# The low parts of the gated delta net's weights: all of them on VectorE

## The chip, the core and the metric

The kernel runs on one core of a Trainium2 chip. The metric is the time of the program on the device, in microseconds. In the profile PE is TensorE's matmuls, PEld its weight loads, DVE is VectorE, ACT is ScalarE, POOL is GpSimd and SP is SyncE, which here only issues DMAs. TensorE's clock has two levels, 2.4 GHz (granted clock 1.0) and 1.2 GHz (0.5).

## What is computed

The reference is a model of four layers on 256 tokens of width 1024. Each layer is a SwiGLU feed-forward part, a mixer, and another feed-forward part; the mixers are an S5, an HGRN2, a gated delta net and a MoBA attention. The change touches the third mixer alone:

```python
def _gdn_mixer(x, w_in, conv_w, a_log, dt_bias, norm_g, w_out):
    qkv, z, beta_raw, a_raw = jnp.split(x @ w_in, [...], axis=-1)
    qkv = jax.nn.silu(_causal_conv(qkv, conv_w))
    q, k, v = jnp.split(qkv, [Hk * dk, 2 * Hk * dk], axis=-1)
    q, k = l2norm(q) * dk ** -0.5, l2norm(k)
    # per chunk: a triangular system, then a scan over the chunks
    sol = triangular_solve(m + eye(C), rhs, lower=True, unit_diagonal=True)
    _, o = lax.scan(step, S0, (...))
    o = _rms(o, norm_g) * jax.nn.silu(z)
    return o @ w_out
```

## The kernel before

Every product with a weight is made from two parts of each factor. A unit of weights is a tile of 128x1024 numbers. It arrives in float32 (`raw`, by SP's DMAs). ScalarE rounds it to TensorE's format (`hi`, line 88), a second engine makes the rest, `lo = raw - hi` (line 91), and TensorE adds up three products, hi by hi, hi by lo and lo by hi. Where the weights are the stationary factor these are lines 315 to 317 (`mm3`, 24 matmuls of 256 columns for a unit), where they move, lines 347 to 349 (`wide`, 12 matmuls of 512 columns).

`Weights.pump` prepares up to four units ahead of the one that TensorE takes next: `hi` and `lo` have four buffers each, and so has `raw`. VectorE makes `lo`, but for units whose number is in the set `aside`: those go to GpSimd. `plan_gdn` puts every second unit of the gated delta net (`GDN_ASIDE = 2`) into that set, 33 of 65.

The gated delta net works in four quarters of four value heads. For each quarter, `project` makes keys and queries (convolution in `conv`, lines 1389 to 1398, tiles `xr`, `cy`, `th`, `kq`; then the norm, an inverse square root of seven to eleven small VectorE instructions on a tile of 128x8, lines 261 to 266 and 1426, tiles `grn_r` and `grn_t`, which TensorE spreads at line 1430). `invert` builds and inverts the triangular matrices (lines 1465 to 1559; GpSimd has four instructions in it, lines 1471, 1477, 1492 and 1508). `values`, `read` (with a second inverse square root, tiles `gf_r` and `gf_t`), `turn`, `gate` and `out` follow. The quarters are interleaved in the code.

The order of the instructions on each engine comes from a scheduler at build time, which goes by its own idea of when things are ready; the code fixes it only where it says `keep_in_program_order`. So a change of the engine of some instructions can give a new order of all the others. On the chip each engine runs its own list in that order.

Of the kernel before, what the change touches and what calls it, by code (L numbers as in the profile page):

```python
# [9 lines left out]
F32 = mybir.dt.float32  # L10
# [3 lines left out]
OP = mybir.AluOpType  # L14
# [5 lines left out]
D_FF = 2816  # L20
FT = D_FF // 128
EPS = 1e-6
GDN_ASIDE = 2
PREP = (2, 16)
WARM = (14, 14, 8)

# [1 line left out]
def as_ap(ap, offset, dims):  # L28
    return bass.AP(tensor=ap.tensor, offset=ap.offset + offset, ap=dims)


class Weights:
# [6 lines left out]
    def __init__(self, nc, raw, split):  # L39
        self.nc, self.raw, self.split = nc, raw, split  # L40
        self.blocks, self.units = [], []
        self.loaded = self.ready = self.taken = 0
        self.tiles, self.parts = {}, {}
        self.aside = set()

    def block(self, srcs, k0, nk, units):

# [28 lines left out]
    def pump(self, most=HL, pin=lambda ins: ins):  # L76
        while True:
            low = min((b for b, _ in self.units[self.ready:self.ready + 8]), default=len(self.blocks))
            if self.loaded < min(len(self.blocks), low + self.RAW):
                self._load()  # L80
            elif self.ready < min(len(self.units), self.taken + most):
                b, (k0, nk, c0, ncol) = self.units[self.ready]
                src = self.tiles[b][:, k0:k0 + nk, c0:c0 + ncol]
                hi = self.split.tile([128, nk * ncol], F32R, tag="hi", name="hi")
                lo = self.split.tile([128, nk * ncol], F32R, tag="lo", name="lo")
                hi = hi.rearrange("p (k c) -> p k c", k=nk)
                lo = lo.rearrange("p (k c) -> p k c", k=nk)
                pin(self.nc.scalar.copy(hi, src))  # L88

                eng = self.nc.gpsimd if self.ready in self.aside else self.nc.vector  # L90
                eng.tensor_tensor(lo, src, hi.bitcast(F32), op=OP.subtract)  # L91
                self.parts[self.ready] = (hi, lo)
                self.ready += 1
            else:
                return
# [8 lines left out]
class Model:  # L104
# [1137 lines left out]

    def plan_gdn(self, i):
        I = self.I
        first = len(self.w.units)
        n = 6176
        w_in = as_ap(I["gdn_w_in"], 0, [[n, D], [1, n]])
        self.w.units += self.w.block([(w_in, n - 128, 128)], 0, KT, [(0, KT, 0, 128)])
        w_out = as_ap(I["gdn_w_out"], 0, [[D, 2 * D], [1, D]])

        def kq(q):
            self.w.cols(w_in, D + q * 256, 256)
            self.w.cols(w_in, q * 256, 256)

        kq(0)
        for q in range(4):
            self.w.cols(w_in, 2 * D + q * 512, 512)
            if q < 3:
                kq(q + 1)
            self.w.wide([(w_in, 4 * D + q * 512, 512)], 0, KT)  # L1260
            if q > 1:
                self.plan_out(w_out, 4 * (q - 2), 4)
        for q in (2, 3):
            self.plan_out(w_out, 4 * q, 4)
        self.w.aside |= set(range(first, len(self.w.units), GDN_ASIDE))

    def gdn_consts(self, pool, i):
        nc, I = self.nc, self.I
# [556 lines left out]
```

## Time and profile before

| | us |
|---|---|
| median of 3 runs | 2255.6 (2252.84 to 2257.62) |
| the profiled execution | 2255.48 |
| its span, first to last instruction | 2253.7 |
| the stretch in which GpSimd makes low parts, 1237 to 1571 us of the span | 334 |

The profiled execution is 0.1 us from the median of the runs, and 1.8 us of it lie outside the span. Over the whole span TensorE is busy 95%, VectorE 65%, ScalarE 51% and GpSimd 13%. A row of groups gives the line, the engine, the operation, tiles as out<-in, shapes, the count, then the busy time in us and the mean of one in ns, then the idle time of that engine just before them and what ended it. A row of waits reads: who waited, for whom, us in all, times, the longest one.

### The profile page before, as it was taken

Reading aid. Unit: us, or ns where it says so; the run is one execution under the profiler, and the core shown is the slowest. Engines: PE = TensorE matmul, PEld = TensorE weight load, DVE = VectorE, ACT = ScalarE, POOL = GpSimd, SP = SyncE. Lnnn points to the kernel's source line nnn. Section 1 sums busy time; section 2 is a strip of 40 time slices with the busy share of each in tenths; the row PEclk is TensorE's granted clock in tenths of the full one; section 3 lists DMA queues with packets and bytes.
Section 4 is the critical chain, followed back from the end, with each engine's and each line's share of the span. In section 5 each row is a group of like instructions: output and inputs, shape, how many; then the busy total and the mean of one; then the engine's idle time right before and its main releaser. Section 6 shows DMA issues by size and latency. Waiting matters only on the chain.

```text
span 2253.7 us, 30309 instructions
## 1 busy us (share of the span) xinstructions
PE 2147.5 (95%) x11480; PEld 1771.5 (79%) x11480; DVE 1464.5 (65%) x2412; ACT 1159.8 (51%) x1876; POOL 288.1 (13%) x305
## 2 busy tenths in 40 slices
PE   8989888999999999999999888899999999999998
PEld 6767566888888888887888766777888888898886
DVE  7986675556555877557554888887655555666555
ACT  6444344445454755445444566764544544555443
POOL 0598600000000000001000422322000000000000
PEclk9999899999999999999999999999999999999999
DMA  8656956655555645555655433233555655555553
GB/s 254 195 188 203 239 185 166 191 195 179 186 179 185 198 132 169 187 190 167 190 185 175 144 100 104 85 113 121 179 187 172 202 186 178 196 168 178 187 177 103
DMA packets 317906, 389.63 MB, mean 173 GB/s; under 512 B 14192, under 2 KB 247856, under 8 KB 316736
## 3 DMA queue, kind: packets, MB, share of 16 engines
q1 hardware_dynamic: 314768, 383.92, 53.7%
q10 hardware_dynamic: 2800, 3.68, 0.9%
q8 instruction: 90, 1.47, 0.3%
q14 instruction: 56, 0.46, 0.1%
q0 software_dynamic: 192, 0.10, 0.0%
HBM read 375.65 MB, written 12.01 MB: 172 GB/s over the span
## 4 chain that ended last, share of the span: by engine, by line
PE 80%; DVE 9%; ACT 4%; DMA 3%; POOL 2%; issue 1%; SPq 0%; ACTq 0%; DVEq 0%; POOLq 0%
PE acc L349 23%; PE acc L347 23%; PE acc L348 23%; DVE lo L91 2%; PE acc L315 2%; PE acc L316 2%; PE acc L317 2%; PE aux L439 2%; DVE cy L1395 1%; DMA raw<-in_ffn_w_up_dram 1%; ACT hi L88 1%; PE aux L230 1%; POOL s5e L733 1%; POOL s5e L734 1%; POOL s5tmp L732 1%
## 5 line engine op out<-in xcount | busy, mean ns | idle before, releaser
L91 DVE TENSOR_TENSOR lo<-raw,hi 128x1024 fp32r<-128x1024 f32 x648 | 813.1, 1257 | 585.4 <-ACT hi L88 582.3
L88 ACT CAST hi<-raw 128x1024 fp32r<-128x1024 f32 x681 | 713.1, 1049 | 708.2 <-PE acc L349 657.5
L347 PE MATMUL acc<-hi,xhl 128*128 128x512 f32 x1568 | 627.2, 400 | 9.9 <-ACT hi L88 9.4
L348 PE MATMUL acc<-lo,xhl 128*128 128x512 f32 x1568 | 618.9, 395 | 2.8 <-DVE lo L91 2.7
L349 PE MATMUL acc<-hi,xhl 128*128 128x512 f32 x1568 | 616.9, 394 | 0.0
L347 PEld LDWEIGHTS acc<-hi,xhl 128*128 128x128 f32 x1568 | 297.1, 190 | 73.0 <-ACT hi L88 10.7
L349 PEld LDWEIGHTS acc<-hi,xhl 128*128 128x128 f32 x1568 | 296.9, 189 | 66.6 <-issue 3.1
L348 PEld LDWEIGHTS acc<-lo,xhl 128*128 128x128 f32 x1568 | 297.5, 190 | 64.4 <-DVE lo L91 5.2
L347 PE MATMUL acc<-hi,hhl 128*128 128x512 f32 x704 | 276.9, 393 | 0.0
L349 PE MATMUL acc<-hi,hhl 128*128 128x512 f32 x704 | 276.7, 393 | 0.0
L348 PE MATMUL acc<-lo,hhl 128*128 128x512 f32 x704 | 275.5, 391 | 0.0
L349 PEld LDWEIGHTS acc<-hi,hhl 128*128 128x128 f32 x704 | 132.8, 189 | 27.6
L348 PEld LDWEIGHTS acc<-lo,hhl 128*128 128x128 f32 x704 | 132.9, 189 | 27.4
L347 PEld LDWEIGHTS acc<-hi,hhl 128*128 128x128 f32 x704 | 132.7, 188 | 27.0
L317 PE MATMUL acc<-xhl,lo 128*128 128x256 f32 x520 | 150.2, 291 | 0.0
L316 PE MATMUL acc<-xhl,hi 128*128 128x256 f32 x520 | 149.5, 290 | 0.2 <-DVE xhl L241 0.2
L315 PE MATMUL acc<-xhl,hi 128*128 128x256 f32 x520 | 149.6, 291 | 0.1
L427 ACT ACTIVATE sl<-acc,norm_r 128x256 f32<-128x256 f32 x176 | 83.6, 475 | 107.2 <-PE acc L349 88.9
L91 POOL TENSOR_TENSOR lo<-raw,hi 128x1024 fp32r<-128x1024 f32 x33 | 81.8, 2478 | 342.7 <-ACT hi L88 322.6
L430 DVE TENSOR_TENSOR h<-acc,sl 128x256 f32<-128x256 f32 x176 | 74.0, 420 | 49.8 <-ACT sl L427 49.7
L315 PEld LDWEIGHTS acc<-xhl,hi 128*128 128x128 f32 x520 | 99.6, 193 | 2.6 <-issue 1.7
L316 PEld LDWEIGHTS acc<-xhl,hi 128*128 128x128 f32 x520 | 99.8, 193 | 1.6 <-issue 0.9
(564 smaller groups left out, 2285.7 us busy)
## 6 DMA issues: line engine op xcount, KB each, us to landing
raw<-in_ffn_w_gate_dram SPq DMA_DIRECT2D x174, 512.0 KB, 3.9
raw<-in_ffn_w_up_dram SPq DMA_DIRECT2D x174, 512.0 KB, 4.8
raw<-in_ffn_w_down_dram SPq DMA_DIRECT2D x80, 1024.0 KB, 4.9
raw<-in_gdn_w_in_dram SPq DMA_DIRECT2D x24, 1024.0 KB, 5.2
raw<-in_hg_w_in_dram SPq DMA_DIRECT2D x16, 1024.0 KB, 5.3
raw<-in_moba_w_in_dram SPq DMA_DIRECT2D x12, 1024.0 KB, 5.0
raw<-in_ffn_w_down_dram SPq DMA_DIRECT2D x16, 512.0 KB, 3.7
raw<-in_s_w_glu_dram SPq DMA_DIRECT2D x16, 512.0 KB, 5.2
```

The costliest lines, as they stand in the source:

```text
L88: pin(self.nc.scalar.copy(hi, src))
L91: eng.tensor_tensor(lo, src, hi.bitcast(F32), op=OP.subtract)
L230: nc.tensor.transpose(q[:, j * 128:j * 128 + 128], self.x[:, t, k * 128:k * 128 + 128], self.ident)
L315: t.matmul(p, hi, ah, start=first, stop=False)
L316: t.matmul(p, hi, al, start=False, stop=False)
L317: t.matmul(p, lo, ah, start=False, stop=last)
L347: mm(p, ah, hi[:, j], start=first and j == 0, stop=False)
L348: mm(p, ah, lo[:, j], start=False, stop=False)
L349: mm(p, al, hi[:, j], start=False, stop=last and j == n - 1)
L427: nc.scalar.activation(sl, p[:, :256], AF.Silu, scale=self.r_col[:, t:t + 1])
L430: return nc.vector.tensor_tensor(waiting[-1][1][:, t], p[:, 256:], sl, op=OP.mult)
L439: nc.tensor.transpose(q[:, c:c + 128], h[:, t, f * 128:f * 128 + 128], self.ident)
```

## The change

The set `aside` and the constant `GDN_ASIDE` go, and line 91 always uses VectorE (it becomes line 87; lines behind it move up by four to six).

```diff
-                eng = self.nc.gpsimd if self.ready in self.aside else self.nc.vector
-                eng.tensor_tensor(lo, src, hi.bitcast(F32), op=OP.subtract)
+                self.nc.vector.tensor_tensor(lo, src, hi.bitcast(F32), op=OP.subtract)
...
     def plan_gdn(self, i):
         I = self.I
-        first = len(self.w.units)
...
-        self.w.aside |= set(range(first, len(self.w.units), GDN_ASIDE))
```

No instruction is added or lost: 33 move from GpSimd's list to VectorE's, and the scheduler orders the gated delta net anew on all engines. Before that stage and behind it the lists are the same.

GpSimd in the middle of the gated delta net, before: low parts (`lo`) stand between the four instructions of `invert` for each quarter.

```order
L91 TENSOR_TENSOR lo<-raw,hi 128x1024 x2
L1508 COPY e<-gd_e 128x256
L1477 TENSOR_TENSOR gd<-gd,beta 128x1024
L91 TENSOR_TENSOR lo<-raw,hi 128x1024 x2
L1492 AFFINE_SELECT nt<-nt 128x1024
L91 TENSOR_TENSOR lo<-raw,hi 128x1024
L1471 AFFINE_SELECT gd<-gd 128x1024
```

The same place now:

```order
L1502 COPY e<-gd_e 128x256
L1471 TENSOR_TENSOR gd<-gd,beta 128x1024
L1486 AFFINE_SELECT nt<-nt 128x1024
L1465 AFFINE_SELECT gd<-gd 128x1024
```

GpSimd keeps four instructions for each quarter, 16 in the stage, and nothing stands between them.

VectorE in the inverse square root of the first quarter's keys and queries, before (`grn_r` and `grn_t` are its small tiles, `cy` is the convolution, and line 1426 is what TensorE's line 1430 waits for):

```order
L265 SCALAR_TENSOR_TENSOR grn_t<-grn_t,gmc 128x8
L1395 SCALAR_TENSOR_TENSOR cy<-xr_10012,gd_w,cy 128x256
L266 SCALAR_TENSOR_TENSOR grn_r<-grn_t,grn_r 128x8
L1395 SCALAR_TENSOR_TENSOR cy<-xr_10012,gd_w,cy 128x256
L264 TENSOR_TENSOR grn_t<-grn_r 128x8
L91 TENSOR_TENSOR lo<-raw,hi 128x1024
L265 SCALAR_TENSOR_TENSOR grn_t<-grn_t,gmc 128x8
L1395 SCALAR_TENSOR_TENSOR cy<-xr_10012,gd_w,cy 128x256
L266 SCALAR_TENSOR_TENSOR grn_r<-grn_t,grn_r 128x8
L1389 TENSOR_TENSOR xr_10012<-acc,r_row 128x256
L1426 TENSOR_SCALAR grn_r<-grn_r 128x8
```

The same stretch now:

```order
L87 TENSOR_TENSOR lo<-raw,hi 128x1024
L261 SCALAR_TENSOR_TENSOR grn_t<-grn_t,gmc 128x8
L1389 SCALAR_TENSOR_TENSOR cy<-xr_10012,gd_w,cy 128x256
L262 SCALAR_TENSOR_TENSOR grn_r<-grn_t,grn_r 128x8
L87 TENSOR_TENSOR lo<-raw,hi 128x1024
L260 TENSOR_TENSOR grn_t<-grn_r 128x8
L1392 SCALAR_TENSOR_TENSOR cy<-th,cy 128x256
L261 SCALAR_TENSOR_TENSOR grn_t<-grn_t,gmc 128x8
L1383 TENSOR_TENSOR xr_10012<-acc,r_row 128x256
L262 SCALAR_TENSOR_TENSOR grn_r<-grn_t,grn_r 128x8
L87 TENSOR_TENSOR lo<-raw,hi 128x1024
L1420 TENSOR_SCALAR grn_r<-grn_r 128x8
```

Three low parts stand in these rows, and a fourth just ahead of them, where one stood in the whole chain; line 1420 is what line 1426 was.

VectorE where the stage begins, before: the residual sum `x` of the feed-forward part ahead and the split of its transposed result `xhl`, which TensorE's first products of the stage read.

```order
L484 SCALAR_TENSOR_TENSOR x<-acc,half,x 128x512
L241 SCALAR_TENSOR_TENSOR xhl<-aux,gains,xhl 128x128 x2
L91 TENSOR_TENSOR lo<-raw,hi 128x1024
L241 SCALAR_TENSOR_TENSOR xhl<-aux,gains,xhl 128x128
L484 SCALAR_TENSOR_TENSOR x<-acc,half,x 128x512
L241 SCALAR_TENSOR_TENSOR xhl<-aux,gains,xhl 128x128
L91 TENSOR_TENSOR lo<-raw,hi 128x1024
```

The same place now:

```order
L480 SCALAR_TENSOR_TENSOR x<-acc,half,x 128x512
L237 SCALAR_TENSOR_TENSOR xhl<-aux,gains,xhl 128x128
L87 TENSOR_TENSOR lo<-raw,hi 128x1024
L237 SCALAR_TENSOR_TENSOR xhl<-aux,gains,xhl 128x128
L87 TENSOR_TENSOR lo<-raw,hi 128x1024
L237 SCALAR_TENSOR_TENSOR xhl<-aux,gains,xhl 128x128
L87 TENSOR_TENSOR lo<-raw,hi 128x1024
L480 SCALAR_TENSOR_TENSOR x<-acc,half,x 128x512
L237 SCALAR_TENSOR_TENSOR xhl<-aux,gains,xhl 128x128
L87 TENSOR_TENSOR lo<-raw,hi 128x1024
```

Three low parts instead of one stand ahead of the second sum of `x`, for which TensorE's transposes wait.

## Rows read from the trace of the kernel before

**Rows 1.** Stretches (us: length, PE, PEld, DVE, ACT, POOL busy; clock, DMA).

```profile
1237.00:1571.00 334.00, 291.96 (x2175) 241.37 (x2174) 272.68 (x567) 206.84 (x453) 101.17 (x49) 0.96 0.34 108
1000.00:1237.00 237.00, 234.74 (x1068) 193.25 (x1067) 134.26 (x205) 114.00 (x157) 6.18 (x13) 1.00 0.57 184
```

**Rows 2.** Waits of TensorE from 1237 to 1571 us.

```profile
PE aux L1430 <- DVE grn_r L1426: 5.9, 2, 4.0
PE aux L1552 <- DVE lo L1547: 5.5, 2, 3.3
...
PE acc L316 <- DVE xhl L241: 0.2, 1, 0.2
```

**Rows 3.** Chain that ended last, 1237 to 1571: shares, longest pieces (start, us, what).

```profile
by line: DVE cy L1395 9.5%; issue 5.5%; PE acc L349 5.1%; PE acc L348 5.1%; PE acc L347 5.0%; DVE lo L91 4.4%; ACT zb L1518 3.3%; ACT hi L88 3.0%; PE aux L1574 2.8%; PE acc L316 2.6%; PE acc L315 2.5%; PE acc L317 2.3%; DVE kq L1398 2.3%; D
...
1293.75 4.12 DVE cy L1395 x4
...
1384.58 3.20 DVE lo L91
```

**Rows 4.** Groups of GpSimd from 1237 to 1571 us, the first.

```profile
L91 POOL TENSOR_TENSOR lo<-raw,hi 128x1024 fp32r<-128x1024 f32 x33 | 81.8, 2478 | 342.7 <-ACT hi L88 322.6 <-PE aux L1516 20.0
```

**Rows 5.** Groups of VectorE from 1237 to 1571 us.

```profile
L1395 DVE SCALAR_TENSOR_TENSOR cy<-xr,gd_w,cy 128x256 f32<-128x256 f32 x96 | 63.3, 666 | 5.0 <-ACT cy L1392 4.4
L91 DVE TENSOR_TENSOR lo<-raw,hi 128x1024 fp32r<-128x1024 f32 x33 | 44.9, 1360 | 8.1 <-ACT hi L88 8.0
...
L1398 DVE SCALAR_TENSOR_TENSOR kq<-th,cy 128x256 f32<-128x256 f32 x16 | 12.6, 786 | 0.6 <-ACT th L1397 0.5
...
L261 DVE TENSOR_SCALAR grn_r<-gmc 128x8 int32<-128x8 int32 x4 | 7.4, 1842 | 0.1
L1398 DVE SCALAR_TENSOR_TENSOR cy<-th,cy 128x256 f32<-128x256 f32 x16 | 7.1, 446 | 2.9 <-ACT th L1397 2.9
...
L262 DVE TENSOR_SCALAR gf_r<-gf_r 128x8 int32<-128x8 int32 x4 | 5.0, 1239 | 0.1
L265 DVE SCALAR_TENSOR_TENSOR gf_t<-gf_t,gm 128x8 f32<-128x8 f32 x12 | 4.2, 346 | 0.2
...
L264 DVE TENSOR_TENSOR grn_t<-grn_r 128x8 f32<-128x8 f32 x12 | 3.6, 297 | 0.2
```

**Rows 6.** The low parts on VectorE from 1000 to 1237 us, ahead of the stage.

```profile
L91 DVE TENSOR_TENSOR lo<-raw,hi 128x1024 fp32r<-128x1024 f32 x81 | 99.1, 1225 | 86.3 <-ACT hi L88 86.2
```

**Rows 7.** VectorE in order of time (start, us, what), from 1272 us.

```profile
1275.03 1.78 DVE L264 TENSOR_TENSOR grn_t<-grn_r 128x8 f32<-128x8 f32 x1
...
1277.45 0.17 DVE L264 TENSOR_TENSOR grn_t<-grn_r 128x8 f32<-128x8 f32 x1
...
1278.46 0.48 DVE L1395 SCALAR_TENSOR_TENSOR cy<-xr,gd_w,cy 128x256 f32<-128x256 f32 x1
...
1278.93 1.22 DVE L91 TENSOR_TENSOR lo<-raw,hi 128x1024 fp32r<-128x1024 f32 x1
1280.07 2.31 DVE L265 SCALAR_TENSOR_TENSOR grn_t<-grn_t,gmc 128x8 f32<-128x8 f32 x1
```

**Rows 8.** GpSimd in order of time, the same place.

```profile
1274.88 1.90 POOL L1477 TENSOR_TENSOR gd<-gd,beta 128x1024 f32<-128x1024 f32 x1
1279.02 3.33 POOL L91 TENSOR_TENSOR lo<-raw,hi 128x1024 fp32r<-128x1024 f32 x1 [2.23 <-ACT hi L88]
```

**Rows 9.** TensorE in order of time, the same place.

```profile
1283.53 0.77 PE L1430 MATMUL aux<-ident,grn_r 128*128 128x128 f32 x2 [4.00 <-DVE grn_r L1426]
```

**Rows 10.** Two stretches with a lower granted clock (the eighth column).

```profile
1280.00:1300.00 20.00, 14.48 (x89) 13.57 (x89) 14.96 (x27) 8.02 (x18) 7.09 (x4) 0.83 0.31 91
...
1440.00:1460.00 20.00, 15.32 (x107) 11.53 (x108) 17.75 (x35) 9.80 (x19) 4.82 (x3) 0.74 0.35 106
```

**Rows 11.** Waits around the parts of the weights, 1237 to 1571 us.

```profile
ACT hi L88 <- PE acc L349: 32.1, 16, 4.8
...
DVE lo L91 <- ACT hi L88: 8.0, 6, 3.1
```

More of the change, by code (lines that the diff above doesn't have):

```diff
@@ L22 @@
 EPS = 1e-6
-GDN_ASIDE = 2
 PREP = (2, 16)
@@ L43, in __init__ @@
         self.tiles, self.parts = {}, {}
-        self.aside = set()
     def block(self, srcs, k0, nk, units):
```

## The prediction

> **What bounds the kernel now.** I read the stretches first, to see which engine has time to give. From 1237 to 1571 us TensorE is idle for 334 - 292.0 = 42.0 us, while in the 237 us ahead of it it is idle for 2.3 us [rows 1]. So a change in this stage can give back some 42 us at most, and what the granted clock hides besides. VectorE is busy 272.7 us there, 82%, more than any engine but TensorE. Next come TensorE's waits, to see who ends them. 13 kinds of them end at a VectorE instruction, and they sum to 32.9 us; the two longest and the shortest are shown [rows 2] (`lo` of line 1547 is a tile of the inversion, not a part of a weight). No wait of TensorE in the stretch ends at a part of a weight, made by either engine. So what TensorE waits for is VectorE's small work on keys, queries and inverses.
>
> Then the groups of VectorE, to see whether it works or stands. The small steps of the inverse square roots have means of 300 to 1840 ns [rows 5], and in order of time one and the same step takes 1.78 us at one place and 0.17 us at another [rows 7]. The step that takes 2.31 us starts at 1280.07 and ends at 1282.38, and GpSimd's low part runs from 1279.02 to 1282.35 [rows 7, 8]. The one that takes 1.78 us ends at 1276.81, and another instruction of GpSimd ends at 1276.78 [rows 7, 8]. So VectorE's instruction is held until GpSimd's ends, and is still counted as busy. TensorE's gap of 4.00 us, up to 1283.53, stands right behind these two [rows 9]. The chain tells the same: its longest pieces in the stretch are such held instructions, at 1293.75 and 1384.58 us for instance [rows 3].
>
> **What the change removes.** The held time, group by group, as busy time less count times the quiet duration: `cy` 63.3 - 96 x 0.48 = 17.2; `kq` 12.6 - 16 x 0.446 = 5.5 (quiet: the other group of the same line); `grn_r` 7.4 - 4 x 0.17 = 6.7; `gf_r` 5.0 - 4 x 0.17 = 4.3; low parts 44.9 - 33 x 1.225 = 4.5; and five groups of twelve small steps each, from 4.2 down to 3.6 us, some 19.8 - 60 x 0.17 = 9.6 [rows 5 to 7]. That is 47.8 us. GpSimd's low parts are 81.8 of its 101.2 busy us there [rows 1, 4], 81%, so 39 us of the held time by share. If the other instructions held nothing it would be 48, but one of them does [rows 8]. I take 42, near the share, since the low parts are also the longest.
>
> The Trainium skill has this as a rule (SBUF — State Buffer, section Who interferes with whom): VectorE and GpSimd share a pair of ports as an exclusive lock, and an instruction of VectorE with two inputs in SBUF is held by one of GpSimd that reads SBUF. By that rule the 16 instructions that GpSimd keeps go on holding VectorE, since they read SBUF too. The trace agrees: the 1.78 us step stood behind one of them. So the 47.8 - 42 us are not counted as gain.
>
> **What it adds.** 33 low parts on VectorE at 1.225 us [rows 6] are 40.4 us; they follow each other at 1.14 us [rows 7], which would make 37.6. I take 40.4. So VectorE's load falls by 42 - 40.4 = 2 us only: it is not relieved. What counts is where the two kinds of time lie.
>
> Held time lies on the path nearly always, because one hold of 2 us puts its own instruction there: I take 90%, 38 us. For low parts the chain has 4.4% of 334 = 14.7 us of the 44.9 that they are busy [rows 3, 5], 33%, which is one bound, 13 us of 40.4; 90%, 36 us, is the other. In the new order three more of them than before stand in the first quarter's inverse square root, which TensorE's line 1430 waits for, so they are nearer to that path than the present ones; I take 60%, 24 us.
>
> A low part on VectorE also waits for its `hi`, and now all of VectorE's list waits with it. The present 33 wait 8.0 us in all [rows 11]. Another 33 at that rate add 8 us of standing, 60% of it on the path: 5 us; the bounds are nothing (the scheduler puts them where `hi` is long done) and 8. GpSimd has such waits today, 322.6 us [rows 4], but that is idle time of an engine with nothing queued behind it except its own four instructions a quarter.
>
> **The clock.** Behind TensorE's gaps the granted clock falls: in three stretches of 20 us it is 0.83, 0.83 and 0.74 (two shown) [rows 10], one of them right behind the gap that ends at 1283.53. Against 1.0 that is 3.4 + 3.4 + 5.2 = 12 us. If the held instructions go and a part of the gaps with them, I count a third back, 4 us; the bounds are 0 and 12.
>
> **What costs nothing.** GpSimd's list gets short; the 16 instructions left start earlier or at the same time. The order of SP's transfers moves in a few places, but no wait of TensorE for weights shows in the stretch. The lists before and behind the stage are unchanged.
>
> **The sum.** -38 + 24 + 5 - 4 = -13 us against the profiled execution, 2255.5, which is as good as the median (2255.6). Forecast: 2242.5 us.
>
> **The rivals.** *The whole gain.* The new low parts lie like the present ones, in the gaps of VectorE's own path: -38 + 13 + 0 - 8 = -33, so 2222 us. For it: TensorE's 32.9 us behind VectorE and the 12 us of clock leave room for it. Against it: the order above shows low parts inside a chain that TensorE waits for.
>
> *An even trade.* VectorE is bound by its load, 82% busy, and its load falls by 2 us while the new order neither helps nor hurts: 2253 us, within 0.2% (4.5 us, about what a measurement of this kernel can tell from no change). For it: the two sums, 42 and 40.4. Against it: it takes held time and low parts for equally harmful, while the chain has 33% of the one and nearly all of the other.
>
> *Slower: VectorE's list stands behind ScalarE's.* ScalarE's `hi` waits for TensorE to free a buffer, 32.1 us in 16 times behind line 349 [rows 11]. With GpSimd out, every such wait passes through `hi` and a low part into VectorE's one list, behind which the convolutions and the inverse square roots queue, and TensorE waits for these. Then 90% of the low parts and all of the standing lie on the path, the clock gives nothing, and the first sum of the stage stands behind three low parts instead of one, 2.4 us: -38 + 36 + 8 + 2.4 = +8.4, so 2264 us. It decides from where over (38 - 8) / 40.4, some three quarters, of the low parts' time lands on the path. For it: the new order puts low parts among the steps of chains. Against it: a low part of 1.2 us is shorter than a hold of some 2 us, and the order puts it where the scheduler thinks `hi` ready, while a hold falls on whatever is just there.
>
> The Trainium skill has a rule that speaks for this side (Perfetto Trace Analysis, section Optimizing Scalar/DVE Operations): with VectorE saturated, giving some of its work even to GpSimd may make sense, though the two share a port and it might not help. By its first half nothing is saved and the added time alone counts, +24 + 5, so 2284 us; the held time in this trace stands against that, and I give it no more than the tail above the range.
>
> That the change doesn't do what it says is out: the new lists show no low part on GpSimd.
>
> **How the numbers follow.** Forecast, from 5 to 24 us faster: 0.42. The whole gain: 0.16. The even trade: 0.20. Slower: 0.22. Faster by over 0.2% is 0.58, within 0.2% is 0.20, slower 0.22. The range reaches to the rivals on both sides, 2222 to 2265, and leaves out about a tenth at either end. The forecast's own range is 2231 to 2250.
>
> **What would show it.** In the profile after: the small steps back at 0.17 us but for a few beside GpSimd's 16 instructions, `cy` near 0.48 and `kq` near 0.45; VectorE's busy time in the stage about the same, with 66 low parts in it; TensorE idle 20 to 30 us instead of 42, and fewer stretches with a lower clock. The forecast is wrong in its main step if the held time goes and TensorE's idle time stays: then low parts stand in the chain of waits where the held steps stood. It is wrong in its first step if the small steps stay long without GpSimd beside them. If VectorE's idle time before low parts grows far beyond 8 + 8 us, the slower rival is at work.

## The result, and the profile after

The changed kernel takes 2225.2 us (median of four runs, 2221.2 to 2227.2), the kernel before in the same comparison 2255.0. The ratio is 0.9865, 95% interval 0.9846 to 0.9884: 30 us faster. The forecast was 13 us faster, 2242.5. The direction and the place were right, and the time lies inside the range, near its lower end; the size was less than half of what came.

The profiled execution took 2227.2 us with a span of 2225.5, 28.2 us under the span before. First the stage and the stretch ahead of it, as in [rows 1] (window, length, busy time of PE, PEld, DVE, ACT and POOL, granted clock, DMA). The window 1239 to 1545 answers to 1237 to 1571 of before.

```profile
1239.00:1545.00 306.00, 287.48 (x2187) 238.51 (x2186) 261.53 (x602) 207.01 (x455) 19.95 (x16) 0.97 0.40 121
```
```profile
1000.00:1239.00 239.00, 236.74 (x1070) 194.66 (x1069) 134.36 (x206) 113.95 (x157) 6.17 (x13) 0.99 0.57 184
```

The whole difference lies in the stage: 334 us became 306. TensorE's idle time there went from 42.0 us to 306 - 287.5 = 18.5, which is 23.5 of the 28; its busy time fell by the other 4.5. The clock accounts for about as much: 0.04 x 334 - 0.03 x 306 = 4.2 us, roughly, since both clocks are rounded to 0.01. The 20 us windows with a lower clock that are left (compare [rows 10]):

```profile
1360.00:1380.00 20.00, 17.41 (x141) 13.20 (x140) 15.96 (x42) 13.55 (x29) 2.51 (x2) 0.83 0.33 105
...
1420.00:1440.00 20.00, 18.31 (x132) 12.01 (x132) 18.25 (x44) 16.13 (x34) 2.52 (x2) 0.86 0.22 62
1440.00:1460.00 20.00, 19.87 (x120) 15.97 (x119) 15.87 (x36) 6.99 (x9) 0.00 (x0) 0.97 0.62 204
...
1520.00:1540.00 20.00, 13.89 (x69) 10.69 (x68) 15.05 (x37) 5.92 (x13) 0.00 (x0) 0.83 0.34 105
```

The window that held the gap of [rows 9] is at 1.00 now. But there are four windows under 1.00, and there were four before: beside the three that the forecast counted there is this one.

```profile
1300.00:1320.00 20.00, 16.15 (x123) 11.44 (x124) 14.52 (x25) 15.55 (x35) 4.76 (x2) 0.92 0.45 145
```

By the forecast's reckoning (what is missing to 1.0, times 20 us) the four lose 10.2 us now and lost 13.6 before. The groups of VectorE and the first of GpSimd in the stage, to be laid beside [rows 4, 5]:

```profile
L87 DVE TENSOR_TENSOR lo<-raw,hi 128x1024 fp32r<-128x1024 f32 x66 | 80.5, 1220 | 8.8 <-ACT hi L86 8.7
L1389 DVE SCALAR_TENSOR_TENSOR cy<-xr,gd_w,cy 128x256 f32<-128x256 f32 x96 | 46.6, 493 | 0.2
...
L1392 DVE SCALAR_TENSOR_TENSOR kq<-th,cy 128x256 f32<-128x256 f32 x16 | 6.9, 430 | 4.4 <-ACT th L1391 4.4
...
L257 DVE TENSOR_SCALAR grn_r<-gmc 128x8 int32<-128x8 int32 x4 | 2.0, 498 | 0.0
...
L262 DVE SCALAR_TENSOR_TENSOR gf_r<-gf_t,gf_r 128x8 f32<-128x8 f32 x12 | 1.8, 154 | 0.1
```
```profile
L1471 POOL TENSOR_TENSOR gd<-gd,beta 128x1024 f32<-128x1024 f32 x4 | 7.6, 1898 | 44.2 <-ACT gd L1470 41.3 <-issue 2.9
```

The groups that were long are back at or near their quiet durations: `cy` 666 to 493 ns, `kq` 786 to 430, the small steps to 154. The `grn_r` of line 257 is the exception, with 498 ns (1842 before): one of its four took 1.52 us and ended at 1275.42, and GpSimd's product with `beta` ended at 1275.39. By the forecast's own reckoning (busy time less count times quiet duration) `cy` keeps 0.5 us of its 17.2 and `grn_r` 1.3 of its 6.7. So VectorE does 33 more low parts in less busy time, 261.5 us for 272.7. Its waits for `hi` are 8.7 us for 66 low parts, where they were 8.0 for 33 [rows 11].

TensorE's waits, all that the view lists (compare [rows 2]), and the chain of the stretch (compare [rows 3]):

```profile
PE aux L1646 <- DVE goo L1643: 6.1, 1, 6.1
PE aux L1516 <- ACT zb L1512: 3.4, 8, 0.7
PE aux L1409 <- ACT csq L1408: 2.8, 3, 1.4
PE aux L1534 <- DVE zz L1530: 2.5, 2, 1.7
PE aux L1357 <- DVE gg L1353: 1.0, 1, 1.0
PE aux L1424 <- DVE grn_r L1420: 1.0, 1, 1.0
PE aux L1439 <- DVE cy L1392: 0.8, 1, 0.8
```
```profile
by line: issue 25.4%; ACT hi L86 6.5%; ACT zb L1512 6.4%; PE acc L343 5.5%; PE acc L345 5.4%; PE acc L344 5.2%; PE acc L311 2.1%; PE acc L312 2.1%; ACT dg L1493 2.0%; PE aux L1568 1.9%; PE acc L313 1.8%; ACT gd L1470 1.8%; ACT gj L1587 1.6%
```

The waits behind VectorE sum to 11.4 us where they were 32.9, and over half of that is one wait for `goo` at the end of the stage. That wait is hardly the low parts' doing: it is still 5.3 us in the run below that leaves all 33 out. No wait ends at a low part. In the chain `cy` led with 9.5% and low parts had 4.4%; now no line of VectorE is among the thirteen of 1.6% and more. Added up piece by piece, low parts have 4.8 us of the chain now, with 66 of them on VectorE, and had 14.6 with 33. But a quarter of this chain is "issue", time whose cause the profile does not show, so that the low parts are nearly off the path has to be shown by runs.

One place says most about the forecast. VectorE's first inverse square root in order of time, then the matmul that waits for it (the 4.00 us gap of [rows 9]):

```profile
1276.54 0.15 DVE L261 SCALAR_TENSOR_TENSOR grn_t<-grn_t,gmc 128x8 f32<-128x8 f32 x1
1276.62 1.21 DVE L87 TENSOR_TENSOR lo<-raw,hi 128x1024 fp32r<-128x1024 f32 x1
...
1278.30 1.21 DVE L87 TENSOR_TENSOR lo<-raw,hi 128x1024 fp32r<-128x1024 f32 x1
...
1279.99 1.21 DVE L87 TENSOR_TENSOR lo<-raw,hi 128x1024 fp32r<-128x1024 f32 x1
1281.13 0.15 DVE L260 TENSOR_TENSOR grn_t<-grn_r 128x8 f32<-128x8 f32 x1
...
1282.03 1.21 DVE L87 TENSOR_TENSOR lo<-raw,hi 128x1024 fp32r<-128x1024 f32 x1
```
```profile
1283.46 1.13 PE L1424 MATMUL aux<-ident,grn_r 128*128 128x128 f32 x8 [0.99 <-DVE grn_r L1420]
```

Four low parts stand inside the chain, three more than before, as the order had shown, and TensorE waits 0.99 us behind it, not 4.00.

### The profile page after: what moved, and what is told of

It is laid out like the page before. It is cut to its first block, busy times and chain, and to the rows that moved or that the text cites. A ratio compares the mean times of both kernels' runs of the same rounds, so it can differ in the third digit from the quotient of the medians.

```text
span 2225.5 us, 30259 instructions
## 1 busy us (share of the span) xinstructions
PE 2142.0 (96%) x11480; PEld 1768.3 (79%) x11480; DVE 1452.5 (65%) x2445; ACT 1159.0 (52%) x1876; POOL 207.8 (9%) x272
## 4 chain that ended last, share of the span: by engine, by line
PE 80%; ACT 5%; DVE 5%; issue 4%; DMA 3%; POOL 2%; SPq 0%; ACTq 0%; POOLq 0%; DVEq 0%
PE acc L343 23%; PE acc L345 23%; PE acc L344 23%; PE acc L311 2%; PE aux L435 2%; PE acc L312 2%; DVE lo L87 2%; PE acc L313 2%; ACT hi L86 1%; DMA raw<-in_ffn_w_up_dram 1%; ACT zb L1512 1%; PE aux L226 1%; POOL s5e L730 1%; POOL s5e L729 1%; POOL s5tmp L728 1%
## 5 line engine op out<-in xcount | busy, mean ns | idle before, releaser
L87 DVE TENSOR_TENSOR lo<-raw,hi 128x1024 fp32r<-128x1024 f32 x681 | 850.0, 1250 | 585.3 <-ACT hi L86 583.6
L313 PEld LDWEIGHTS acc<-xhl,lo 128*128 128x128 f32 x520 | 100.1, 193 | 2.0 <-DVE lo L87 1.0
```

The costliest lines, as they stand in the source:

```text
L87: self.nc.vector.tensor_tensor(lo, src, hi.bitcast(F32), op=OP.subtract)
L313: t.matmul(p, lo, ah, start=False, stop=last)
```

## The experiments

All but one of the runs keep an order: edges without a semaphore tie each instruction to the one ahead of it on TensorE, VectorE, ScalarE and SyncE, in the order that the scheduler made for the changed kernel (or for the kernel before, where it says so). What is added or left out then moves nothing else, except a few VectorE instructions at the edge of the stage. The 33 low parts themselves, and what is added, are not tied: the scheduler places them between the others.

```
def pin(tc, nc):
    made = {i.name: i for i in nc.cur_bb.bb.instructions}
    ...
                    tc.add_manual_dep(i, last.name, mybir.DependencyInfo(
                        mybir.DependencyClass.NoSync, mybir.DependencyReason.DATA), reason="order")
```

The expectations work with differences of medians. Below, "against the changed kernel" is the difference of the two ratios to before, times 2255 us, since the runs were made on several chips. With intervals of 0.001 to 0.002 on each ratio, a difference of less than some 5 us is not told from nothing.

| run | median us | ratio to before, interval | us against the changed kernel |
|---|---|---|---|
| changed kernel | 2225.2 | 0.9865, 0.9846 to 0.9884 | 0 |
| gpsimd_new_order | 2247.6 | 0.9972, 0.9961 to 0.9984 | +24.1 |
| vector_old_order | 2227.9 | 0.9882, 0.9867 to 0.9897 | +3.8 |
| gpsimd_fills_new_order | 2218.7 | 0.9841, 0.9825 to 0.9858 | -5.4 |
| gpsimd_reads_new_order | 2258.0 | 1.0011, 1.0002 to 1.0020 | +32.9 |
| half_aside | 2238.6 | 0.9923, 0.9907 to 0.9939 | +13.1 |
| none_all | 2222.0 | 0.9849, 0.9832 to 0.9866 | -3.6 |
| none_half | 2223.0 | 0.9855, 0.9836 to 0.9874 | -2.3 |
| twice_half | 2240.2 | 0.9935, 0.9920 to 0.9949 | +15.8 |
| vector_twice | 2252.0 | 0.9979, 0.9969 to 0.9989 | +25.7 |
| vector_spare | 2249.9 | 0.9978, 0.9968 to 0.9988 | +25.5 |
| beta_vector | 2230.9 | 0.9888, 0.9874 to 0.9903 | +5.2 |
| beta_pinned | 2224.0 | 0.9864, 0.9850 to 0.9879 | -0.2 |

### The engine or the order?

The change does two things: another engine makes the low parts, and the scheduler makes another order. These two runs are the two crossed cases.

```
 gpsimd_new_order: the kernel before, with the order of the changed kernel
 vector_old_order: the changed kernel, with the order of the kernel before
+            pin(tc, nc)
```

> GpSimd makes the 33 low parts as before, but every instruction of TensorE, ScalarE and SyncE, and of VectorE without those 33, is pinned to the order of the changed kernel. Theory of the held instructions (GpSimd's low parts hold VectorE, and that is what the change took away): the time is that of the kernel before, 2248 to 2262 us, with some 40 to 50 us of held time on VectorE's small steps. Theory of the order (the scheduler's new order is what helped, whoever makes the low parts): 2220 to 2232 us. A time between them gives each its share.

> VectorE makes all low parts, but TensorE, ScalarE, SyncE and VectorE's other instructions are pinned to the order of the kernel before; the 33 low parts are slotted into VectorE's list. Theory of the held instructions: 2222 to 2235 us, the steps of the inverse square roots back at 0.17 us. Theory of the order: 2248 to 2262 us, although nothing is held.

With the low parts on GpSimd the new order gives 0.28%, 6.3 us; the 2247.6 us lie just under the 2248 that the theory of the held instructions named. With the new engine the old order gives 0.9882, 26.6 of the 30 us. So the engine makes most of the gain in either order (26.6 us in the old, 24.1 in the new), and the order some 4 to 6, of which only the case on GpSimd is clear of its interval. Low parts back on GpSimd (first row) bring the held time back, whatever the order (second row, VectorE's `cy`, which took 493):

```profile
L91 POOL TENSOR_TENSOR lo<-raw,hi 128x1024 fp32r<-128x1024 f32 x33 | 83.1, 2519 | 309.2 <-ACT hi L88 292.6 <-issue 9.8 <-PE acc L349 6.8
```
```profile
L1395 DVE SCALAR_TENSOR_TENSOR cy<-xr,gd_w,cy 128x256 f32<-128x256 f32 x96 | 66.3, 699 | 0.4
```

### What the holds cost, and what the low parts cost

```
-                eng = self.nc.gpsimd if self.ready in self.aside else self.nc.vector
-                eng.tensor_tensor(lo, src, hi.bitcast(F32), op=OP.subtract)
+                if self.ready in self.aside:
+                    self.nc.gpsimd.memset(lo.bitcast(F32), 0.001)
+                else:
+                    self.nc.vector.tensor_tensor(lo, src, hi.bitcast(F32), op=OP.subtract)
```

> Order of the changed kernel, pinned. For the 33 units nobody subtracts: GpSimd fills the low part with a constant, which reads no memory, so that part of the result is left out. It prices the 33 low parts on VectorE. As the prediction had it (60% of them and of their waits on the path, 29 us): 2190 to 2202 us. If low parts on VectorE lie beside the path: 2215 to 2227 us. Both theories agree that VectorE's steps are not held if a GpSimd instruction that only writes does not hold; if writing holds too, the steps are long again and the time lies above 2230 us.

GpSimd still has 33 instructions on the same tiles, but they read nothing and neither engine makes those low parts (first row GpSimd, second VectorE):

```profile
L91 POOL MEMSET lo<- 128x1024 f32 x33 | 31.4, 954 | 322.3 <-PE acc L350 251.7 <-PE acc L319 70.6
```
```profile
L1397 DVE SCALAR_TENSOR_TENSOR cy<-xr,gd_w,cy 128x256 f32<-128x256 f32 x96 | 46.9, 495 | 1.0 <-ACT cy L1394 0.5
```

`cy` stays at 495 ns: an instruction of GpSimd that only writes does not hold it. Against GpSimd making the low parts in the same order, this run is (0.9972 - 0.9841) x 2255 = 29.5 us faster: the price of the holds, with what the clock loses by them. The same stretch of gpsimd_new_order, then of this run, in the columns of [rows 1]:

```profile
1233.00:1570.00 337.00, 299.48 (x2230) 247.41 (x2229) 281.60 (x579) 215.97 (x471) 102.97 (x49) 0.96 0.37 115
```
```profile
1233.00:1542.00 309.00, 292.37 (x2229) 243.37 (x2228) 234.29 (x579) 214.29 (x471) 50.31 (x49) 0.98 0.40 125
```

VectorE has the same 579 instructions in both and is busy for 281.6 - 234.3 = 47.3 us less here. So 47.3 us of held time cost 29.5 us of the kernel, 62%.

Two other readings of the 29.5 us would be that low parts made by GpSimd come late, or that GpSimd's own four instructions a quarter queue behind them. The traces speak against both. Neither in the kernel before nor in gpsimd_new_order does another engine wait for a low part of GpSimd. And the waits of the other engines for GpSimd's own instructions, all of them ScalarE's, are as short with low parts on GpSimd as without: 5.0 us in the kernel before, 4.5 in gpsimd_new_order, 4.5 in this run, 5.2 in the changed kernel.

Against the changed kernel this run is 5.4 us faster: the price of 33 low parts on VectorE, which the forecast put at 29. The two intervals overlap, so 5.4 is hardly told from zero.

The other way round, the changed kernel with reads of GpSimd that nobody needs, two of half size for each of the 33 low parts, into a spare tile:

```
+                    for j in range(2):
+                        c = slice(j * nk // 2, (j + 1) * nk // 2)
...
+                        self.nc.gpsimd.tensor_tensor(d, src[:, c], hi[:, c].bitcast(F32), op=OP.subtract)
```

> The changed kernel with its own order pinned, VectorE making all low parts, and besides it GpSimd makes 33 useless ones, each in two halves, into a spare tile nobody reads. Theory of the held instructions: nothing waits for GpSimd, yet VectorE is held again: 25 to 45 us longer than the changed kernel, 2250 to 2270 us, and more time on VectorE than before. Theory of the order: 2222 to 2230 us, since no list but GpSimd's changes.

```profile
L96 POOL TENSOR_TENSOR spare<-raw,hi 128x512 bf16<-128x512 f32 x66 | 104.9, 1589 | 324.9 <-ACT hi L89 180.9 <-issue 140.9 <-POOL spare L96 0.4
```
```profile
L91 DVE TENSOR_TENSOR lo<-raw,hi 128x1024 fp32r<-128x1024 f32 x68 | 92.1, 1354 | 8.2 <-ACT hi L89 8.0
L1401 DVE SCALAR_TENSOR_TENSOR cy<-xr,gd_w,cy 128x256 f32<-128x256 f32 x96 | 55.3, 584 | 1.1 <-ACT cy L1398 0.9
```

Nobody reads these results, no wait of TensorE's matmuls ends at them, and they cost 32.9 us, more than the change had gained: `cy` is up to 584 ns again and a low part to 1354. The spare reads also keep `raw` and `hi` in use a little longer, which this run does not separate; the run below with the same reads on VectorE bears on it.

Half of the low parts back on GpSimd, 17 of 33 (`GDN_ASIDE = 4`), order kept:

> GpSimd makes 17 of the 33 low parts (every fourth unit instead of every second), VectorE the other 16, with the order of the changed kernel kept. Theory (each GpSimd read that meets VectorE costs by itself): half of the 22.4 us between GpSimd making all 33 in this order and none, 10 to 13 us over the changed kernel, so 2235 to 2239 us, with some 28 us of held time. Rival one (there is room for some holds, only many hurt): 2226 to 2231. Rival two (a few badly placed holds make nearly all of the loss): 2242 to 2248.

```profile
L91 POOL TENSOR_TENSOR lo<-raw,hi 128x1024 fp32r<-128x1024 f32 x17 | 43.6, 2567 | 303.4 <-ACT hi L88 294.5 <-PE aux L1516 8.9
```
```profile
L1395 DVE SCALAR_TENSOR_TENSOR cy<-xr,gd_w,cy 128x256 f32<-128x256 f32 x96 | 57.1, 603 | 0.3
```

With none, 17 and 33 low parts on GpSimd the kernel stands at 0, +13.1 and +24.1 us: 0.77 and 0.73 us for each, and `cy` (second row) lies midway, at 603 ns between 493 and 699. The loss grows in proportion; it is not a few unlucky places.

### Why so cheap on VectorE: room, until it is used up

```
 vector_twice (33 of them), twice_half (17, GDN_ASIDE = 4)
                 self.nc.vector.tensor_tensor(lo, src, hi.bitcast(F32), op=OP.subtract)
+                if self.ready in self.aside:
+                    self.nc.vector.tensor_tensor(lo, src, hi.bitcast(F32), op=OP.subtract)
```

> VectorE makes each of the 33 low parts twice in succession, into the same buffer, with the order of the changed kernel kept on TensorE, ScalarE and SyncE and otherwise on VectorE: 33 x 1.22 = 40 us more work for VectorE, nothing more for GpSimd. Theory (VectorE has slack, and a low part does not sit on the path): the second 33 cost about what the first 33 did, 6.5 us, so 2229 to 2236 us, and the low parts in the chain of waits stay under 10 us. Rival (the first 33 were cheap because they just used up the slack; VectorE stands still for 47.6 us in the stage of the changed kernel, and 40 more fill it): the forecast's price comes back, 24 us or more, so 2246 to 2260.

This went against my theory and for its rival: the second 33 cost 25.7 us, 0.78 each, where the first had cost some 5. VectorE's two groups of low parts, TensorE's longest wait and the chain of the stage:

```profile
L91 DVE TENSOR_TENSOR lo<-raw,hi 128x1024 fp32r<-128x1024 f32 x68 | 83.1, 1223 | 7.4 <-ACT hi L89 7.4
...
L93 DVE TENSOR_TENSOR lo<-raw,hi 128x1024 fp32r<-128x1024 f32 x33 | 40.1, 1214 | 0.0
```
```profile
PE acc L350 <- DVE lo L93: 9.1, 4, 4.5
```
```profile
by line: issue 14.2%; DVE lo L91 9.4%; DVE lo L93 6.3%; DVE cy L1397 5.1%; PE acc L350 4.1%; PE acc L349 3.8%; PE acc L351 3.6%; ACT zb L1520 2.0%; DVE gr L1577 1.5%; DVE xr L1391 1.4%; PE aux L1486 1.4%; PE aux L1654 1.4%; DVE x L1668 1.2%
```

VectorE is back on the chain without any holds: low parts have 15.7% of it. TensorE waits behind the second copies, so a rival reading was that the weights came later. The next run takes that away by putting the useless half-size subtractions of the run above on VectorE instead of GpSimd, behind the low part, where nobody awaits them:

```
-                        self.nc.gpsimd.tensor_tensor(d, src[:, c], hi[:, c].bitcast(F32), op=OP.subtract)
+                        self.nc.vector.tensor_tensor(d, src[:, c], hi[:, c].bitcast(F32), op=OP.subtract)
```

> The changed kernel, order kept, with the 66 useless half-size subtractions of the earlier run now on VectorE in place of GpSimd: two behind each of the 33 low parts, into a spare buffer that nobody reads; some 33 x 1.3 = 43 us of work for VectorE. Making the low parts twice cost 26.7 us, and 9.1 us of TensorE's waits stood behind the second copies. Theory one (VectorE's load is the limit: the work of the changed kernel fills what slack there was): 25 to 30 us over the changed kernel, so 2250 to 2256, as much as the second copies although no weight comes later. Theory two (the second copies cost because the weights came later, the load itself hides): 8 to 18 us, so 2233 to 2243. On GpSimd the same instructions cost 32.8 us.

```profile
L96 DVE TENSOR_TENSOR spare<-raw,hi 128x512 bf16<-128x512 f32 x66 | 45.1, 684 | 0.1
```
```profile
PE aux L1421 <- ACT csq L1420: 7.6, 3, 5.2
PE aux L1658 <- DVE goo L1655: 7.4, 2, 7.1
PE acc L354 <- DVE lo L91: 4.5, 1, 4.5
PE aux L1436 <- DVE grn_r L1432: 3.2, 2, 2.8
```

The price is the same, 25.5 us, while TensorE's waits for low parts fall from 9.1 us to 4.5 and others take their place. So most of it is the work added to VectorE, wherever TensorE then waits, and not the lateness of weights. The same instructions on GpSimd cost 7.4 us more than here.

> As the run that made 33 low parts twice, but only 17 of them: 21 us more work for VectorE. The first 33 low parts cost 6.5 us, the 33 second copies 26.7. If the price grows with the load, this one lies between: 17 copies at a price between 0.2 and 0.8 us each, 3.5 to 14 us. Theory one (every second copy costs the same, because it is what stands in succession that hurts): 26.7 x 17 / 33 = 13.8, so 2237 to 2241. Theory two (slack is used up step by step): 5 to 9 us, so 2230 to 2234.

17 second copies cost 15.8 us, 0.93 each: theory one or a little over, not the gentle slope of theory two. But theory one's reason, that the copies stand in succession, does not hold as it was put: in the trace of vector_twice some second copies stand three to nine other instructions of VectorE behind the low part ahead of them.

The last two runs look at the other side, with low parts left out and no fill in their place (TensorE takes the high part where the low one should stand):

```
+                if self.ready in self.aside:
+                    lo = hi
...
```

> The 33 low parts are left out altogether (TensorE takes the high part in their place, so the output is not the reference's), with the order of the changed kernel kept. The run in which GpSimd filled those tiles with a constant was 6.5 us faster than the changed kernel; it still had 50 us of GpSimd work and fills that TensorE had to await. Theory one (VectorE had room for 33 low parts, and the price rises only beyond them): about as that run, 2215 to 2220 us. Theory two (each low part costs about 0.8 us at any load, as the second copies do, and the fills themselves hid it): 33 x 0.8 = 27 us less than the changed kernel, 2196 to 2202.

> As the run without the 33 low parts, but only 17 of them left out and VectorE makes the other 16, with the order of the changed kernel kept. Theory one (the price rises with the load): 17 of the last low parts cost 4 to 6 us and the first 16 next to nothing, so 2219 to 2222 us. Theory two (each costs about the same): half of what leaving all out gives.

Theory one held in both, though the times lie 2 us and 1 us above what it named: 3.6 us less with all 33 gone, 2.3 with 17 gone. The stage of the changed kernel, then that of none_all, then that of vector_twice, in the columns of [rows 1]; the stretch is some 10 us longer here, so that the three hold nearly the same matmuls:

```profile
1237.00:1552.00 315.00, 296.48 (x2230) 245.90 (x2229) 267.35 (x613) 214.16 (x471) 19.95 (x16) 0.97 0.40 123
```
```profile
1239.00:1550.00 311.00, 294.91 (x2228) 246.26 (x2228) 233.06 (x579) 214.20 (x471) 19.05 (x16) 0.97 0.39 124
```
```profile
1234.00:1577.00 343.00, 305.37 (x2232) 251.79 (x2231) 300.81 (x645) 215.26 (x471) 20.99 (x16) 0.95 0.36 113
```

With none of the 33, VectorE stands still for 311 - 233.1 = 77.9 us, and TensorE is still idle for 16.1, where the changed kernel has 18.5: what is left of its idle time is hardly VectorE's load. The longest of its waits in none_all is the one for `goo`:

```profile
PE aux L1656 <- DVE goo L1653: 5.3, 1, 5.3
```

That wait comes with the new order: in the old one, with the same low parts on VectorE, `goo` costs 2.5 us in two waits. With 33 too many TensorE's idle time is 37.6.

So the price of low parts on VectorE has a bend. With 0, 16, 33, 50 and 66 of them beyond the 33 that were always there, the kernel stands at -3.6, -2.3, 0, +15.8 and +25.7 us. Up to 33 one costs about 0.1 us, beyond it 0.8 to 0.9. The bend lies at or just above the changed kernel's load. Why just there is open: all other instructions keep an order that was made without the further ones, and a run in which the scheduler orders everything anew for 50 was not made. That 33 low parts put into the old order, which was made with them on GpSimd, cost only 3.8 us more than in the new one speaks against the order as the main cause.

### Going further

GpSimd's product with `beta`, 4 x 1.9 us, is the longest instruction that it keeps, and it reads two inputs. This run is the one in which the scheduler made its own order.

```
-                nc.gpsimd.tensor_tensor(d, d, beta[:, :, hs].unsqueeze(3).to_broadcast([128, 2, 4, 128]), op=OP.mult)
+                nc.vector.tensor_tensor(d, d, beta[:, :, hs].unsqueeze(3).to_broadcast([128, 2, 4, 128]), op=OP.mult)
```

> The changed kernel with one more step taken from GpSimd: the product with beta, 4 instructions of 128x1024 that read two inputs and take 1.9 us each, goes to VectorE. Theory: the 5.9 us of held time that are left fall to some 2 us, and 4 x 1.2 us of work are added at a place that TensorE's inverse waits for: the sum is within 3 us of the changed kernel, 2222 to 2228. Rival (holds weigh more than work, as with the low parts: 28.9 against 6.5 us for 33): 3 to 5 us faster, 2220 to 2222. Rival (the order moves with it and that decides): up to 8 us either way.

> The product with beta on VectorE, as in the earlier run (5.7 us slower than the changed kernel), but with the changed kernel's order kept on TensorE, ScalarE and SyncE and otherwise on VectorE. If the order that the scheduler made for it was the cause, this one is 2222 to 2227, as the changed kernel or a little faster by the held time that goes; if the four instructions themselves are the cause (they stand on the path to the inverse, 1.2 us each, where GpSimd's 1.9 us ran beside it), 2227 to 2232.

By itself it was slower, 2230.9 us; in the changed kernel's order it took 2224.0, as fast as the changed kernel and no faster. So the move gains nothing: what the four instructions cost on VectorE and what the held time gives back are not told apart here. The difference between the two runs is the order's, 5.4 us by the ratios, whose intervals just overlap. No full version was found that clearly beats the changed kernel.

## Why the prediction came out as it did

**What bounds the kernel** was read rightly. Held instructions of VectorE, for which TensorE waited, cost the time, and the long small steps of [rows 5, 7] were the sign of it. Giving the reads back costs it again, with no one waiting for them.

**What the change removes**, -38 for the holds and -4 for the clock, was some 12 us too large: the runs give 29.5 for both in one order. The held time itself was sized well (47.8 us read, 42 of them to go; 47.3 measured), but 62% of it lay on the path, clock included, where 90% was taken. The new order, for which the sum had no term, gave 6.3, so that the side removed came to 36 in place of 42. The 4 us of the clock agree with TensorE's busy time, which fell by 4.5.

**What the change adds** is the step that failed, and most of the miss: "I take 60%, 24 us" and the 5 us for `hi`. The 33 low parts cost 5.4 us by the run with fills and 3.6 by the run without them, in place of 29. The 60% lay between two bounds, both read from the chain of before. I read it so: in that chain VectorE was late because of the holds, and so whatever stood on it was on the path; once the holds went, VectorE was ahead again, and 1.2 us more at a place was taken out of its lead. A lead is not seen in a trace as such; what the traces show is the low parts' piece of the chain, 14.6 us of 44.9 before and 4.8 of 80.5 after. So a share of the chain of before could not be carried over, since the change itself removed what had put the engine there. The lower bound, 13 us, was still above what came. The reason that moved me up from it, the three low parts in the first inverse square root, was true of the order and wrong of the time: TensorE's wait there fell from 4.00 us to 0.99.

**The waits for `hi`** were to grow by 8 us and grew by 0.7 [rows 11], so nearly all of the 5 us for them is a part of that excess. In all the forecast missed by 17 us: 6 too much on the side removed, some 23 too much on the side added.

**The rivals.** The whole gain (2222 us, chance 0.16) is what happened, by its own reason: the low parts lie beside the path. It deserved the larger chance. That its time came within some 3 us is partly luck: its sum took 46 us off and put 13 on, where the runs give 36 and 5. The even trade took VectorE to be bound by its load at 82%; the runs show that it is not at this load, and that it is with 17 low parts more. The slower case needed three quarters of the low parts' time on the path; about an eighth (5.4 of 40.4) came to lie there. Its mechanism, VectorE's list standing behind ScalarE's `hi`, shows in none of these runs as a large wait: VectorE waits 8.7 us for `hi` in the changed kernel and 7.4 with 33 second copies. In that last run TensorE waits 9.1 us for low parts themselves. The rule of the Trainium skill that spoke for it (Perfetto Trace Analysis, Optimizing Scalar/DVE Operations), that giving work even to GpSimd may make sense where VectorE is saturated, spoke for the kernel before; its own reservation, that the two share a port and it might not help, is what came here, by 24.1 us in one order. The Trainium skill's rule on the port pair (SBUF — State Buffer, Who interferes with whom) says besides that VectorE's instruction with two inputs does not contend with a GpSimd instruction that only writes. The runs agree: `cy` took 495 ns beside 33 fills, and 699 beside 33 reads.

**What would show it** was right in its signs: small steps quiet, VectorE's busy time about the same, TensorE idle for less (18.5 us, just under the 20 to 30 named). One sign did not come: the windows with a lower clock are four, as before, and only a little less deep.

## What to carry to other kernels

Where one engine's instructions of the same shape have very different durations, look for another engine's instruction that ends with the long ones, and count its price in the held engine's path, not in its own time: an engine that nobody waits for can be the most costly one. When you cost work that an engine takes over, do not read its share of the path from a trace in which that engine is late for the reason that you are removing; ask how much lead it will have afterwards, and test the load on both sides, since the price can bend. Compare with the order kept before you credit or blame an instruction, because here a scheduler's new order alone moved the time by some 4 to 6 us.

## What the runs showed of the hardware that was not expected

GpSimd's reads cost more than their size says. A subtraction of half the size took 1589 ns beside VectorE, 64% of the 2478 ns of a whole one [rows 4], while the same half-size instruction on VectorE took 684 ns, 56% of its whole one's 1220 (the halves write bf16, the whole ones fp32r); 66 halves kept GpSimd busy for 104.9 us and VectorE for 45.1. Whether GpSimd was itself held there by VectorE, these runs do not separate. And a constant fill of the whole tile took GpSimd 954 ns and left VectorE's instructions as they were.
